# Long convolutions by FFT: the GpSimd instructions moved to the vector engine, two frequency halves joined in one operation

## The chip, the cores and the metric

The kernel runs on one core of a Trainium2 chip. A core has TensorE (PE: matmuls; its weight loads are shown as PEld), VectorE (DVE), ScalarE (ACT), GpSimd (POOL) and SyncE (SP, which here issues nearly all DMAs). Each engine executes its own instructions strictly in the order in which they stand; waits between engines go over semaphores. The metric is the device time of one execution in microseconds. Everything is float32; products that must be exact are formed as three matmuls of split operands.

## The reference, cut to what matters

One layer of a diffusion transformer for 1024 latent tokens and 256 context tokens: input projection, eight attention heads, beside them a Hyena group of 512 channels with two long convolutions in a row, output projection, feed-forward layer. The convolutions are what the change touches:

```python
def _long_conv(u, k_f, bias):
    L = u.shape[1]
    uf = u.astype(jnp.float32)
    y = jnp.fft.irfft(jnp.fft.rfft(uf, n=2 * L, axis=1) * k_f[None], n=2 * L, axis=1)[:, :L]
    return (y + uf * bias.astype(jnp.float32)).astype(u.dtype)

def _hyena(hy, k_f, filt_bias):
    x1, x2, v = jnp.split(hy, 3, axis=-1)
    z = x1 * _long_conv(v, k_f[:, 0], filt_bias[0])
    return x2 * _long_conv(z, k_f[:, 1], filt_bias[1])
```

## The kernel before, in words

The stages in order of time: filters and input projections (to 591 us), attention (first scores at 629 us, last product at 916 us), output projection, feed-forward up and down. The long convolutions, `chain(j)`, lie over the end of the projections and over attention. There are five chains: j = 0 to 3 are 128 latent channels each ("latent chains"), j = 4 is the context with all its channels. Each has two passes, o = 0 and o = 1, one for each convolution in a row; the second needs the result of the first.

A latent pass does this: a forward transform as 8 matmuls (L802) into PSUM tiles `cA`; twiddles, two on ACT (L814, L815) and one on DVE (L816); a butterfly over the four residues (L823 to L828) from tile `Gt` to `X`; the product with the filter spectrum `K` (L837 to L844), which is loaded in two halves into one buffer, so that the second half's load waits until both products of the first half have read; a second butterfly (L849 to L854); twiddles again (L858 to L860); an inverse transform as 8 matmuls (L872); products with the gates (L877 to L885). Pass 1 ends with a store to `hyd`. The index `h` (0, 1) is the half of the 256 frequencies, `i` the real and imaginary part, `q` the residue. Chain 4 has no butterflies and twiddles: ACT copies the transform (L805), and the products follow.

Before the change, part of this is done on GpSimd: L823 for h = 1, L828 for h = 0, the first product L841, three of six steps of the second butterfly (L849, L853, L854), the sum L879 and the last product L885.

The order of the instructions on each engine is not written out. The program is recorded, and a scheduler that plays the program through with a cost model of its own (`schedule_with_timeline_sim=True`) sets the order on all engines together; `chain` is recorded after the projections with a raised priority (`tc.high_priority(offset=CHP)`). So a change of an engine or of an operation's size also changes the places of instructions that are not touched. Chains 0 and 1 have three PSUM banks `cA`, chains 2 to 4 have one.

Attention works on pairs of heads p = 0 to 3: scores (L1021), addition of the bias table `tb` with a row maximum on DVE (L1042), exponentials on ACT (L1055, L1056), transposes (L1065) that DVE and ACT copy in turn (L969, L971), products with the values (L979), scaling into `at` (L1111). The bias tables are loaded by SP with 96 small DMAs for each pair. After attention the load of `w_out` (`wor`, L1149) takes over the memory of the chains and stands on SP behind the last store of `hyd` (L893). In the changed program the lines after L822 have numbers lower by one (L841 is L840, L872 is L871, L1111 is L1110); lines of the first butterfly are L822 to L827.

Of the kernel before, what the change touches and what calls it, by code (L numbers as in the profile page):

```python
# [86 lines left out]
def _build(nc, tc, top, V, A, G, T, Q, I, O, dbg, upto):  # L87
# [20 lines left out]
    def bk(tag):  # L108
        pl, n, bufs = banks[tag]
        return pl.tile([P, 512 * n], F32, tag=tag, name="ps" + tag, bufs=bufs)  # L110
# [22 lines left out]
    def tw_chain(h, r):  # L133
        b = (h * 3 + r - 1) * 3
        return tw[:, b:b + 1], tw[:, b + 1:b + 2], tw[:, b + 2:b + 3]
# [364 lines left out]
    with ies:  # L500
# [3 lines left out]
        for gi, (s, col, tl) in enumerate(groups):  # L504
            xs = []
# [264 lines left out]
    def chain(j):  # L770

        lat = j < 4
        b_ = j % 2

        def s8():
            return cp.tile([P, 2048], F32, tag=f"s8{b_}", name="s8", bufs=2)

        def s4(dt=F32):
            return cp.tile([P, 1024], dt, tag=f"s4{b_}", name="s4", bufs=S4B)

        f4 = "p (h i q c) -> p h i q c"
        v2 = "p (i x) -> p i x"
        src = lxd[j] if lat else cxd
        f1 = "p i x -> p (i x)"

        def load(which):
            t = s4()
            Q.dma_start(out=t, in_=src[which].rearrange(f1))
            return t

        u = load(0)
        for o in range(2):
            uv = u.rearrange(v2, i=2)
            Gt = s8()
            Gv = Gt.rearrange(f4, h=2, i=2, q=4)
            for h in range(2):
                hs = slice(h * P, (h + 1) * P)
                for rp in range(2):
                    pa = bk("cA")
                    xs = slice(rp * 256, (rp + 1) * 256)  # L800
                    for i in range(2):
                        T.matmul(pa[:, i * 256:(i + 1) * 256], dftf[:, i, hs], uv[:, i, xs], start=True, stop=True)  # L802
                    pv = pa.rearrange("p (i r c) -> p i r c", i=2, r=2)
                    if not lat:
                        A.copy(Gv[:, h, :, 2 * rp:2 * rp + 2], pv)  # L805
                        continue
                    for ri in range(2):
                        r = 2 * rp + ri
                        if r == 0:
                            A.copy(Gv[:, h, :, 0], pv[:, :, 0])  # L810
                            continue
                        c, s, ns = tw_chain(h, r)
                        t = cp.tile([P, 2, P], F32, tag=f"t{b_}", name="t", bufs=TB)
                        A.activation(t[:, 0], pv[:, 1, ri], AF.Copy, scale=ns)  # L814
                        A.activation(t[:, 1], pv[:, 0, ri], AF.Copy, scale=s)  # L815
                        V.scalar_tensor_tensor(Gv[:, h, :, r], pv[:, :, ri], c, t, op0=ALU.mult, op1=ALU.add)  # L816
            if lat:
                ac = s4().rearrange(f4, h=2, i=2, q=2)
                X = s8()
                Xv = X.rearrange(f4, h=2, i=2, q=4)  # L820
                Xf = X.rearrange("p (h x c) -> p h x c", h=2, x=8)
                for h in range(2):  # L822
                    (G if h else V).tensor_add(ac[:, h], Gv[:, h, :, 0:2], Gv[:, h, :, 2:4])  # L823
                    V.tensor_sub(Gv[:, h, :, 2:4], Gv[:, h, :, 0:2], Gv[:, h, :, 2:4])
                    V.tensor_sub(Xf[:, h, 2:8:5], Gv[:, h, :, 2], Gv[:, h, ::-1, 3])
                    V.tensor_add(Xf[:, h, 3:7:3], Gv[:, h, :, 2], Gv[:, h, ::-1, 3])
                    V.tensor_add(Xv[:, h, :, 0], ac[:, h, :, 0], ac[:, h, :, 1])  # L827
                    (V if h else G).tensor_sub(Xv[:, h, :, 1], ac[:, h, :, 0], ac[:, h, :, 1])  # L828
                Y = Gt
            else:  # L830
                X = Gt
                Y = s8()
            Xs = X.rearrange("p (h i x) -> p h i x", h=2, i=2)
            Ys = Y.rearrange("p (h i x) -> p h i x", h=2, i=2)
            for h in range(2):
                Kt = cp.tile([P, 2, 512], F32, tag=f"K{b_}", name="K", bufs=1)
                Q.dma_start(out=Kt.rearrange(f1), in_=(Kd[o, j] if lat else Kc[o])[:, h * 1024:(h + 1) * 1024])  # L837
                kr = Kt[:, 0:1].to_broadcast([P, 2, 512])
                ki = Kt[:, 1:2].to_broadcast([P, 2, 512])
                B = s4().rearrange(v2, i=2)  # L840
                G.tensor_mul(B, Xs[:, h, ::-1], ki)  # L841
                V.tensor_mul(Ys[:, h], Xs[:, h], kr)
                V.tensor_sub(Ys[:, h, 0], Ys[:, h, 0], B[:, 0])
                V.tensor_add(Ys[:, h, 1], Ys[:, h, 1], B[:, 1])  # L844
            if lat:
                ac = s4().rearrange(f4, h=2, i=2, q=2)
                Gf = Gt.rearrange("p (h x c) -> p h x c", h=2, x=8)
                for h in range(2):
                    G.tensor_add(ac[:, h], Gv[:, h, :, 0:4:2], Gv[:, h, :, 1:4:2])  # L849
                    V.tensor_sub(Xv[:, h, :, 0:2], Gv[:, h, :, 0:4:2], Gv[:, h, :, 1:4:2])  # L850
                    V.tensor_add(Gf[:, h, 1:8:6], Xv[:, h, :, 0], Xv[:, h, ::-1, 1])
                    V.tensor_sub(Gf[:, h, 3:6:2], Xv[:, h, :, 0], Xv[:, h, ::-1, 1])
                    G.tensor_add(Gv[:, h, :, 0], ac[:, h, :, 0], ac[:, h, :, 1])  # L853
                    G.tensor_sub(Gv[:, h, :, 2], ac[:, h, :, 0], ac[:, h, :, 1])  # L854
                    for r in (1, 2, 3):
                        c, s, ns = tw_chain(h, r)
                        t = cp.tile([P, 2, P], F32, tag=f"t{b_}", name="t", bufs=TB)
                        A.activation(t[:, 0], Gv[:, h, 1, r], AF.Copy, scale=s)  # L858
                        A.activation(t[:, 1], Gv[:, h, 0, r], AF.Copy, scale=ns)
                        V.scalar_tensor_tensor(Gv[:, h, :, r], Gv[:, h, :, r], c, t, op0=ALU.mult, op1=ALU.add)  # L860
            if o == 0:
                x1 = load(1).rearrange(v2, i=2)
                un = s4()
            else:
                x2 = load(2).rearrange(v2, i=2)
                ot = s4().rearrange(v2, i=2)
            for rp in range(2):
                pa = bk("cA")
                xs = slice(rp * 256, (rp + 1) * 256)
                for i in range(2):  # L870
                    for h in range(2):  # L871
                        T.matmul(pa[:, i * 256:(i + 1) * 256], idft[:, i, h], Ys[:, h, i, xs], start=h == 0,  # L872
                                 stop=h == 1, skip_group_check=True)
                pv = pa.rearrange(v2, i=2)
                tt = cp.tile([P, 2, 2, 256], F32, tag=f"s4{b_}", name="tt", bufs=S4B)
                if o == 0:
                    V.tensor_mul(tt[:, 0], pv, x1[:, :, xs])  # L877
                    V.tensor_mul(tt[:, 1], pv, x1[:, ::-1, xs])
                    G.tensor_add(un.rearrange(v2, i=2)[:, :, xs], tt[:, :, 0], tt[:, :, 1])  # L879
                else:  # L880
                    yt = tt[:, 0, 0]
                    A.copy(yt, pv[:, 0])
                    V.tensor_sub(ot[:, 0, xs], yt, pv[:, 1])
                    V.tensor_add(ot[:, 1, xs], yt, pv[:, 1])
                    G.tensor_mul(ot[:, :, xs], ot[:, :, xs], x2[:, :, xs])  # L885
            if o == 0:
                u = un
            elif lat:
                for i in range(2):
                    Q.dma_start(out=hyd[i * 4:i * 4 + 4, :, j * P:(j + 1) * P].rearrange("r p c -> p r c"),  # L890
                                in_=ot[:, i].rearrange("p (r c) -> p r c", r=4))
            else:
                Q.dma_start(out=hyd[8:10].rearrange("i p x -> p i x"), in_=ot)  # L893

    for j in range(5):
        if j == 2:
            cbk.close()
            cbk = Banks("bkd", "right", "tile", cA=(1, 1))
        with tc.high_priority(offset=CHP):
            chain(j)  # L900
# [319 lines left out]
    ot = wo_.tile([P, 512], F32, tag="ot", name="ot", bufs=1)  # L1220
# [296 lines left out]
    for f in range(NFF):  # L1517
# [7 lines left out]
        i, cs = f // 2, slice(f % 2 * 256, f % 2 * 256 + 256)  # L1525
# [77 lines left out]
    B = {(r, b): wdn[:, :, r, b] for r in range(2) for b in range(2)}  # L1603
# [53 lines left out]
    xs = {}  # L1657
# [107 lines left out]
```

## Time and profile before

| | us |
|---|---|
| median of three runs (lowest, highest) | 1921.23 (1920.3, 1921.35) |
| the profiled execution | 1918.35 |
| its span, first to last instruction | 1916.6 |
| busy: PE, DVE, ACT, POOL | 1748.7, 1372.6, 885.0, 412.4 |
| mean granted clock of TensorE | 0.947 |

In the profile a row of a group gives line, engine, operation, result and operands by the names of the program, shapes and count; then busy time in us and mean duration in ns; then the idle time of the engine just before, and what ended it. A row of the timeline starts with the start and the duration in us and may end with the idle time before it and its releaser in brackets. A row of stretches gives start and end, length, and the busy time (with the number of instructions) of PE, PEld, DVE, ACT and POOL, then the granted clock, the share of DMA and GB/s. A row of waits names who waited for whom: us in total, times, longest. A matmul of 128x256 shows as two records (x4 is two matmuls).

### The profile page before, as it was taken

To read this page: it belongs to the slowest core of one execution; us is meant where nothing else is said; L and a number is where in the kernel's file an instruction comes from. 1 tells how busy PE (TensorE), PEld (TensorE's weight loads), DVE (VectorE), ACT (ScalarE), POOL (GpSimd) and SP (SyncE) were. 2 spreads that over 40 slices of the span, in tenths; PEclk is the share of its full clock that TensorE was granted. 3 is DMA by queue.
4 is the path that set the end of the run, shared out by engine and by line. 5 is a ranking of instruction groups with operands and counts; after the bars stand their busy time and mean duration, and the time that the engine had idled before them with its cause. 6 is when DMAs were issued, how large, how long until landed. Compare 5 with 4: busy or idle time off the path is not lost.

```text
span 1916.6 us, 27816 instructions
## 1 busy us (share of the span) xinstructions
PE 1748.7 (91%) x9999; PEld 1468.5 (77%) x9999; DVE 1372.6 (72%) x2175; ACT 885.0 (46%) x1827; POOL 412.4 (22%) x331
## 2 busy tenths in 40 slices
PE   5899989999994789789899699999999999999998
PEld 1688877887773345445688599999999999788786
DVE  4667648747777776776455888888877777656887
ACT  4654435434333355455555544444444444443352
POOL 2354546543654322233100000000000000000001
PEclk7999989999997799799899799999999999999999
DMA  7424444455433334421622154555322222853663
GB/s 266 133 75 129 130 128 119 143 170 170 139 111 122 84 96 94 108 63 56 209 99 100 57 161 163 164 168 173 114 72 73 72 62 71 286 184 109 207 209 127
DMA packets 238267, 249.80 MB, mean 130 GB/s; under 512 B 56610, under 2 KB 187795, under 8 KB 237873
## 3 DMA queue, kind: packets, MB, share of 16 engines
q1 hardware_dynamic: 236168, 247.09, 41.2%
q8 instruction: 79, 1.29, 0.3%
q10 hardware_dynamic: 1705, 0.82, 0.2%
q14 instruction: 59, 0.48, 0.1%
q0 software_dynamic: 256, 0.11, 0.0%
HBM read 176.75 MB, written 71.20 MB: 129 GB/s over the span
## 4 chain that ended last, share of the span: by engine, by line
PE 36%; DVE 10%; DMA 6%; issue 3%; ACT 3%; POOL 1%; SPq 0%; DVEq 0%; POOLq 0%; ACTq 0%
PE psd L118 6%; PE psd L116 6%; PE psd L117 6%; PE psa L116 2%; PE psa L117 2%; PE psa L118 2%; DMA wt<-in_w_down_dram 2%; DMA tdr<-wt 2%; PE psc L117 1%; PE psc L118 1%; PE psc L116 1%; PE psb L117 1%; PE psb L118 1%; PE psb L116 1%; DVE cv L1514 1%
## 5 line engine op out<-in xcount | busy, mean ns | idle before, releaser
L116 PE MATMUL psp<-hh,wh 128*128 128x512 f32 (+1 forms) x552 | 203.1, 368 | 2.3 <-ACT wh L121 1.9
L117 PE MATMUL psp<-hl,wh 128*128 128x512 f32 (+1 forms) x552 | 201.1, 364 | 0.0
L118 PE MATMUL psp<-hh,wl 128*128 128x512 f32 (+1 forms) x552 | 200.3, 363 | 0.0
L1680 POOL TENSOR_TENSOR rs<-rs,mhalf 128x1 f32<-128x1 f32 x10 | 7.7, 770 | 812.5 <-DVE rs L1679 812.5
L116 PE MATMUL psa<-T,ws 128*128 128x256 f32 (+1 forms) x528 | 166.1, 315 | 3.1 <-ACT rows L1480 3.0
L117 PE MATMUL psa<-T,ws 128*128 128x256 f32 (+1 forms) x528 | 165.6, 314 | 2.8 <-DVE T L1207 2.8
L118 PE MATMUL psa<-T,ws 128*128 128x256 f32 (+1 forms) x528 | 165.0, 313 | 0.0
L116 PE MATMUL psd<-wd,gs 128*128 128x512 f32 x360 | 140.5, 391 | 3.1 <-ACT gs L121 3.1
L117 PE MATMUL psd<-wd,gs 128*128 128x512 f32 x360 | 140.9, 391 | 0.0
L118 PE MATMUL psd<-wd,gs 128*128 128x512 f32 x360 | 124.9, 390 | 1.6 <-DVE gs L122 1.6
L116 PEld LDWEIGHTS psp<-hh,wh 128*128 128x128 f32 x552 | 106.5, 193 | 23.7 <-issue 7.0
L117 PEld LDWEIGHTS psp<-hl,wh 128*128 128x128 f32 x552 | 106.7, 193 | 15.0 <-issue 1.2
L116 PE MATMUL psc<-T,ws 128*128 128x384 f32 (+1 forms) x352 | 110.3, 313 | 8.4 <-ACT ws L121 8.4
L118 PEld LDWEIGHTS psp<-hh,wl 128*128 128x128 f32 x552 | 106.0, 192 | 14.9 <-issue 0.8
L117 PE MATMUL psc<-T,ws 128*128 128x384 f32 (+1 forms) x352 | 110.3, 313 | 0.0
L118 PE MATMUL psc<-T,ws 128*128 128x384 f32 (+1 forms) x352 | 110.1, 313 | 0.0
L117 PE MATMUL psb<-T,ws 128*128 128x384 f32 (+1 forms) x352 | 109.7, 312 | 0.0
L118 PE MATMUL psb<-T,ws 128*128 128x384 f32 (+1 forms) x352 | 109.6, 311 | 0.0
L116 PE MATMUL psb<-T,ws 128*128 128x384 f32 (+1 forms) x352 | 109.5, 311 | 0.0
L116 PEld LDWEIGHTS psa<-T,ws 128*128 128x128 f32 x528 | 101.4, 192 | 4.6 <-ACT rows L1480 4.5
L117 PEld LDWEIGHTS psa<-T,ws 128*128 128x128 f32 x528 | 101.5, 192 | 3.1 <-DVE T L1207 3.1
L118 PEld LDWEIGHTS psa<-T,ws 128*128 128x128 f32 x528 | 101.1, 192 | 0.0
(391 smaller groups left out, 4821.2 us busy)
## 6 DMA issues: line engine op xcount, KB each, us to landing
wada<-in_w_ada_dram SPq DMA_DIRECT2D x48, 512.0 KB
wr<-in_w_up_dram SPq DMA_DIRECT2D x44, 512.0 KB
gr<-gdr SPq DMA_DIRECT2D x44, 320.0 KB
wr<-in_w_in_dram SPq DMA_DIRECT2D x23, 512.0 KB
wt<-in_w_down_dram SPq DMA_DIRECT2D x44, 256.0 KB
tdr<-wt SPq DMA_DIRECT2D x44, 256.0 KB
gdr<-cv SPq DMA_DIRECT2D x22, 512.0 KB
wr<-tdr SPq DMA_DIRECT2D x20, 512.0 KB
```

Source lines behind the costliest of these rows:

```text
L116: T.matmul(out, ah, bh, start=start, stop=False, skip_group_check=True)
L117: T.matmul(out, ah, bl, start=False, stop=False, skip_group_check=True)
L118: T.matmul(out, al, bh, start=False, stop=stop, skip_group_check=True)
L1514: V.scalar_tensor_tensor(cv, r[:, 2:NC + 2], ffw(2, ch), cv, op0=ALU.mult, op1=ALU.add)
L1680: G.tensor_tensor(rs, rs, mhalf, op=ALU.pow)
```

## The change

All instructions of `chain` that ran on GpSimd are issued on VectorE, and in both butterflies of a latent pass the loop over the two halves h is gone: one operation of twice the size takes both. The loop over h remains for the product with `K` and for the twiddles behind the second butterfly.

```diff
-                for h in range(2):
-                    (G if h else V).tensor_add(ac[:, h], Gv[:, h, :, 0:2], Gv[:, h, :, 2:4])
-                    V.tensor_sub(Gv[:, h, :, 2:4], Gv[:, h, :, 0:2], Gv[:, h, :, 2:4])
-                    V.tensor_sub(Xf[:, h, 2:8:5], Gv[:, h, :, 2], Gv[:, h, ::-1, 3])
-                    V.tensor_add(Xf[:, h, 3:7:3], Gv[:, h, :, 2], Gv[:, h, ::-1, 3])
-                    V.tensor_add(Xv[:, h, :, 0], ac[:, h, :, 0], ac[:, h, :, 1])
-                    (V if h else G).tensor_sub(Xv[:, h, :, 1], ac[:, h, :, 0], ac[:, h, :, 1])
+                V.tensor_add(ac, Gv[:, :, :, 0:2], Gv[:, :, :, 2:4])
+                V.tensor_sub(Gv[:, :, :, 2:4], Gv[:, :, :, 0:2], Gv[:, :, :, 2:4])
+                V.tensor_sub(Xf[:, :, 2:8:5], Gv[:, :, :, 2], Gv[:, :, ::-1, 3])
+                V.tensor_add(Xf[:, :, 3:7:3], Gv[:, :, :, 2], Gv[:, :, ::-1, 3])
+                V.tensor_add(Xv[:, :, :, 0], ac[:, :, :, 0], ac[:, :, :, 1])
+                V.tensor_sub(Xv[:, :, :, 1], ac[:, :, :, 0], ac[:, :, :, 1])
...
-                G.tensor_mul(B, Xs[:, h, ::-1], ki)
+                V.tensor_mul(B, Xs[:, h, ::-1], ki)
...
+                V.tensor_add(ac, Gv[:, :, :, 0:4:2], Gv[:, :, :, 1:4:2])
+                V.tensor_sub(Xv[:, :, :, 0:2], Gv[:, :, :, 0:4:2], Gv[:, :, :, 1:4:2])
+                V.tensor_add(Gf[:, :, 1:8:6], Xv[:, :, :, 0], Xv[:, :, ::-1, 1])
+                V.tensor_sub(Gf[:, :, 3:6:2], Xv[:, :, :, 0], Xv[:, :, ::-1, 1])
+                V.tensor_add(Gv[:, :, :, 0], ac[:, :, :, 0], ac[:, :, :, 1])
+                V.tensor_sub(Gv[:, :, :, 2], ac[:, :, :, 0], ac[:, :, :, 1])
                 for h in range(2):
-                    G.tensor_add(ac[:, h], Gv[:, h, :, 0:4:2], Gv[:, h, :, 1:4:2])
-                    V.tensor_sub(Xv[:, h, :, 0:2], Gv[:, h, :, 0:4:2], Gv[:, h, :, 1:4:2])
-                    V.tensor_add(Gf[:, h, 1:8:6], Xv[:, h, :, 0], Xv[:, h, ::-1, 1])
-                    V.tensor_sub(Gf[:, h, 3:6:2], Xv[:, h, :, 0], Xv[:, h, ::-1, 1])
-                    G.tensor_add(Gv[:, h, :, 0], ac[:, h, :, 0], ac[:, h, :, 1])
-                    G.tensor_sub(Gv[:, h, :, 2], ac[:, h, :, 0], ac[:, h, :, 1])
...
-                    G.tensor_add(un.rearrange(v2, i=2)[:, :, xs], tt[:, :, 0], tt[:, :, 1])
+                    V.tensor_add(un.rearrange(v2, i=2)[:, :, xs], tt[:, :, 0], tt[:, :, 1])
...
-                    G.tensor_mul(ot[:, :, xs], ot[:, :, xs], x2[:, :, xs])
+                    V.tensor_mul(ot[:, :, xs], ot[:, :, xs], x2[:, :, xs])
```

The program has 8 instructions more on DVE (2185 for 2177) and 104 fewer on POOL (229 for 333); PE, ACT and SP have the same instructions in another order.

The first place is PE at the end of the attention, before the change. `pscA` are the transforms of the chains (L802 forward, L872 inverse), `psX` transposes and row scalings of attention, `psav` its products with the values; L1170 begins the stage that follows.

```order
L872 MATMUL pscA<-s_6432,idft 128x256 x4
L979 MATMUL psav<-pt,vs 64x256 x2
L1065 MATMUL psX<-ident,Pl_6518 128x128 x2
L1065 MATMUL psX<-ident,Pl_6522 128x128 x2
L979 MATMUL psav<-pt,vs 64x256 x2
L989 MATMUL psX<-ident,lrow_6500 128x128
...
L994 MATMUL psX<-lt,sel 128x128 x4
L1170 MATMUL psX<-ones_71,asq 128x2
```

And the same place in the changed program:

```order
L871 MATMUL pscA<-s_6147,idft 128x256 x4
L978 MATMUL psav<-pt,vs 64x256 x2
L988 MATMUL psX<-ident,lrow_6404 128x128
...
L993 MATMUL psX<-lt,sel 128x128 x4
L1169 MATMUL psX<-ones_71,asq 128x2
L1169 MATMUL psX<-ones_71,sq 128x2
...
L802 MATMUL pscA<-s_6264,dftf 128x256 x8
L871 MATMUL pscA<-s_6283,idft 128x256 x8
L802 MATMUL pscA<-s_6300,dftf 128x256 x8
L871 MATMUL pscA<-s_6336,idft 128x256 x8
L1169 MATMUL psX<-ones_71,asq 128x2
```

Before, the first row is the end of chain 4, and attention matmuls stand behind it. Now the first row is the end of chain 3, and all four transforms of chain 4 stand together behind the last matmul of attention.

The second place is DVE at the same moment, first before the change (`at` is attention's last product, `tt` and `s` belong to chain 4), then in the changed program.

```order
L883 TENSOR_TENSOR s_6449<-tt,pscA 128x256
L884 TENSOR_TENSOR s_6449<-tt,pscA 128x256
L1111 TENSOR_TENSOR at_6483<-psav,bs 128x2x16x16
L1136 COPY sh_8562<-mods 128x16
L1173 TENSOR_SCALAR ria<-psX 128x2
```

```order
L884 TENSOR_TENSOR s_6241<-s_6241,s_6239 128x2x256
L1110 TENSOR_TENSOR at_6387<-psav,bs 128x2x16x16
L840 TENSOR_TENSOR s_6286<-s_6266,K 128x1024
L841 TENSOR_TENSOR s_6283<-s_6266,K 128x1024
L842 TENSOR_TENSOR s_6283<-s_6283,s_6286 128x512
L843 TENSOR_TENSOR s_6283<-s_6283,s_6286 128x512
...
L882 TENSOR_TENSOR s_6353<-tt,pscA 128x256
L883 TENSOR_TENSOR s_6353<-tt,pscA 128x256
L884 TENSOR_TENSOR s_6353<-s_6353,s_6351 128x2x256
L1135 COPY sh_8466<-mods 128x16
```

All 28 DVE instructions of chain 4, from the first product with K to the last gate, now stand behind attention's last product.

The third place is PE where the projections (`psp`) end and attention begins (`psS`, scores); the chains here are chain 1 (and one forward transform of chain 2, right ahead of the scores). Before:

```order
L118 MATMUL psp<-hh,wl 128x256
L225 MATMUL pstB<-wada_7_5270,silc 32x256 x4
...
L677 MATMUL pstB<-ident,fo 128x128 x2
L732 MATMUL pstB<-ident,ck 128x128 x2
L872 MATMUL pscA<-s_5715,idft 128x256 x8
L802 MATMUL pscA<-s_5848,dftf 128x256 x2
L1021 MATMUL psS<-k,q 128x264 x2
```

And now:

```order
L118 MATMUL psp<-hh,wl 128x256
L871 MATMUL pscA<-s_5566,idft 128x256
...
L871 MATMUL pscA<-s_5566,idft 128x256 x3
L677 MATMUL pstB<-ident,fo 128x128 x2
L871 MATMUL pscA<-s_5566,idft 128x256 x3
L802 MATMUL pscA<-s_5660,dftf 128x256 x2
L732 MATMUL pstB<-ident,ck 128x128 x2
L802 MATMUL pscA<-s_5660,dftf 128x256 x6
L871 MATMUL pscA<-s_5679,idft 128x256 x8
L802 MATMUL pscA<-s_5800,dftf 128x256 x2
L1020 MATMUL psS<-k,q 128x264 x2
```

Before, only the inverse transform of chain 1's pass 1 stands between projections and scores. Now the inverse transform of its pass 0 and the forward transform of its pass 1 stand there as well.

## The prediction

> **What bounds the kernel now.** I read the page first, then the busy time by stretches, then the waits of PE, then the timeline around the places where the changed lines stand.
>
> ```profile
> span 1916.6 us, 27816 instructions
> PE 1748.7 (91%) x9999; PEld 1468.5 (77%) x9999; DVE 1372.6 (72%) x2175; ACT 885.0 (46%) x1827; POOL 412.4 (22%) x331
> ```
>
> PE is the bound of the whole, but the long convolutions run from 436 to 913 us, beside the end of the input projections and the whole attention. There the stretches differ (PE, PEld, DVE, ACT, POOL busy, then the granted clock):
>
> ```profile
> 440.00:591.00 151.00, 140.47 (x738) 113.71 (x736) 115.42 (x164) 55.91 (x132) 79.19 (x51) 0.94 0.40 123
> 600.00:628.90 28.90, 8.31 (x22) 5.00 (x22) 20.09 (x34) 5.32 (x15) 17.85 (x32) 0.57 0.50 145
> 628.90:728.60 99.70, 76.67 (x394) 43.52 (x393) 78.86 (x177) 48.81 (x167) 32.47 (x23) 0.85 0.39 96
> 728.60:769.90 41.30, 38.38 (x258) 24.41 (x257) 26.31 (x52) 26.43 (x83) 6.19 (x5) 1.00 0.40 97
> 769.90:848.90 79.00, 58.63 (x321) 34.14 (x321) 58.70 (x123) 38.32 (x125) 28.08 (x20) 0.85 0.36 89
> 848.90:915.80 66.90, 63.52 (x373) 39.65 (x373) 42.38 (x97) 35.44 (x109) 21.32 (x10) 0.97 0.18 56
> ```
>
> The first row is the projections, the second the gap before attention, the other four the head pairs 0 to 3. PE is full in the projections and in pairs 1 and 3, and has holes in the gap and in pairs 0 and 2. What PE waits for in the first two stretches:
>
> ```profile
> PE pscA L872 <- POOL s L853: 3.6, 1, 3.6
> PE pscA L872 <- DVE s L860: 3.1, 2, 2.6
> PE pscA L872 <- DVE s L860: 15.9, 2, 14.4
> ```
>
> The first two rows are from 440 to 591 us, the third from 600 to 630. So GpSimd is rarely what PE waits for directly; what it does to Vector shows in the groups (busy us, mean ns):
>
> ```profile
> L842 DVE TENSOR_TENSOR s<-s,K 128x1024 f32<-128x1024 f32 x20 | 41.1, 2055 | 4.0 <-DMA K<-Kc 3.2 <-ACT s L805 0.5
> L844 DVE TENSOR_TENSOR s<-s,s 128x512 f32<-128x512 f32 x20 | 22.9, 1143 | 0.0
> L843 DVE TENSOR_TENSOR s<-s,s 128x512 f32<-128x512 f32 x20 | 21.1, 1053 | 11.7 <-POOL s L841 11.6
> L850 DVE TENSOR_TENSOR s<-s 128x512 f32<-128x512 f32 x16 | 14.8, 926 | 0.0
> L824 DVE TENSOR_TENSOR s<-s 128x512 f32<-128x512 f32 x16 | 12.9, 806 | 2.4 <-POOL s L823 2.2
> ...
> L841 POOL TENSOR_TENSOR s<-s,K 128x1024 f32<-128x1024 f32 x20 | 58.6, 2929 | 58.0 <-DVE s L826 18.3 <-ACT s L805 16.6 <-issue 11.8
> L849 POOL TENSOR_TENSOR s<-s 128x512 f32<-128x512 f32 x16 | 24.4, 1527 | 0.6 <-DVE s L844 0.6
> L885 POOL TENSOR_TENSOR s<-s,s 128x512 f32<-128x512 f32 x10 | 13.1, 1312 | 58.3 <-issue 42.5 <-DVE s L884 15.8
> ```
>
> **Part 1, the work that moves to Vector.** Undisturbed prices on Vector, and what surrounds them at the end of attention:
>
> ```profile
> 893.39 1.22 DVE L842 TENSOR_TENSOR s<-s,K 128x1024 f32<-128x1024 f32 x1 [0.20 <-ACT s L805]
> 896.88 0.69 DVE L843 TENSOR_TENSOR s<-s,s 128x512 f32<-128x512 f32 x1 [0.33 <-POOL s L841]
> 896.77 1.13 PE L802 MATMUL pscA<-s,dftf 128*128 128x256 f32 x4
> 897.94 0.59 ACT L805 COPY s<-pscA 128x512 f32<-128x512 f32 x1 [1.00 <-PE pscA L802]
> 896.87 3.75 DMA K<-Kc
> 900.78 3.37 POOL L841 TENSOR_TENSOR s<-s,K 128x1024 f32<-128x1024 f32 x1 [3.93 <-DMA K<-Kc]
> 906.81 0.37 ACT L882 COPY tt<-pscA 128x256 f32<-128x256 f32 x1 [1.87 <-PE pscA L872]
> 907.22 0.42 DVE L883 TENSOR_TENSOR s<-tt,pscA 128x256 f32<-128x256 f32 x1 [1.05 <-ACT tt L882]
> 908.91 1.89 PE L872 MATMUL pscA<-s,idft 128*128 128x256 f32 x8
> 912.12 1.27 POOL L885 TENSOR_TENSOR s<-s,s 128x512 f32<-128x512 f32 x1 [2.75 <-DVE s L884]
> 913.41 2.78 DMA hyd<-s
> 915.14 0.69 DVE L1111 TENSOR_TENSOR at<-psav,bs 128x512 f32<-128x512 f32 x1 [3.10 <-ACT bs L996]
> 916.33 0.81 SPq L1149 DMA_DIRECT2D wor<-in_w_out_dram  x2
> ```
>
> So 1024, 512 and 256 elements cost 1.22, 0.69 and 0.42 us. What GpSimd did becomes, at these prices, 20 x 1.22 (L841) + 16 x 0.69 (L849) + 32 x 0.42 (L853, L854) + 8 x 0.69 (L823) + 8 x 0.42 (L828) + 20 x 0.69 (L879, L885) = 71.5 us. Each joined pair saves about 0.15 us (2 x 0.69 - 1.22, 2 x 0.42 - 0.69); 12 pairs in 8 latent passes give 14.5. Vector gets 57 us more. Against it stands the stretch: the five Vector rows above hold 112.8 us, and 40 operations at 0.69, 20 at 1.22 and 32 at 0.69 would be 74, so 39 us vanish with GpSimd's work. Vector's own load rises by at most 18 us over 475; smaller groups that are stretched too may bring that to nothing. It is no gain in itself, and no loss: what decides is where the work stands now.
>
> **Part 2, the start of attention.** The rows of the order show that the inverse transform of pass 0 of chain 1 no longer stands inside the projections: 8 + 8 + 8 matmuls of chain 1 now come after the last projection matmul.
>
> ```profile
> 590.85 0.28 PE L118 MATMUL psp<-hh,wl 128*128 128x256 f32 x1
> 618.24 1.19 PE L872 MATMUL pscA<-s,idft 128*128 128x256 f32 x2 [14.39 <-DVE s L860]
> 623.01 0.48 DVE L860 SCALAR_TENSOR_TENSOR s<-s,tw,t 128x256 f32<-128x256 f32 x1 [0.89 <-ACT t L859]
> 628.91 1.20 PE L1021 MATMUL psS<-k,q 64*128 64x264 f32 x8
> ```
>
> The projections get shorter by the waits of 3.6 and 3.1 us and by 16 matmuls of 0.53 (a row of x4 is two matmuls, 1.03 to 1.13 us): 15 us. From their end to the first scores it was 38 us. Now the serial list is: three last twiddles at 1.4 (0.48 and the wait of 0.89 for ACT), two inverse blocks at 1.9 with their products at 1.4 and a sum, 12; a forward transform and six twiddles, a little under 8; butterfly 2 x 1.22 + 4 x 0.69 = 5; products 2 x (2 x 1.22 + 2 x 0.69) = 7.6, and between them the reload of K of 3.9, of which 1.4 lies behind the two subtractions, 10; butterfly 5; six twiddles at 1.4, 8; inverse transform 2 and the forward one ahead of the scores 1: about 50 us. So 15 less and 12 more. I take 0; from -12 (the memsets of GpSimd no longer delay the butterfly) to +12 (Vector, held by the K reload, keeps the projections' results waiting).
>
> **Part 3, attention with one chain less.** Chain 4 (the context) leaves pair 3, where PE is busy 63.5 of 66.9 us. Its 32 matmuls at 0.53 are 17 us. Another 3 us I take from Vector's waits for GpSimd in attention:
>
> ```profile
> DVE s L843 <- POOL s L841: 6.7, 7, 1.8
> ...
> L842 DVE TENSOR_TENSOR s<-s,K 128x1024 f32<-128x1024 f32 x12 | 23.1, 1927 | 3.9 <-DMA K<-Kc 3.2 <-ACT s L805 0.5
> L843 DVE TENSOR_TENSOR s<-s,s 128x512 f32<-128x512 f32 x12 | 10.6, 882 | 6.8 <-POOL s L841 6.7
> L844 DVE TENSOR_TENSOR s<-s,s 128x512 f32<-128x512 f32 x12 | 10.3, 859 | 0.0
> ```
>
> Together -20 (half of that wait, since PE has holes only in two pairs of four). At best the whole wait and the stretch of these three rows (44.0 less 12 x 1.22 and 24 x 0.69, 13 us) come off the holes of pairs 0 and 2: -37. At worst Vector's added work lands in the holes and the gain of PE is lost behind it: +8.
>
> **Part 4, the tail.** In the changed order chain 4 stands whole after the last attention product, on PE, ACT and DVE alike. Before, it ended (912.12 + 1.27 = 913.4) 2.4 us ahead of attention (915.14 + 0.69 = 915.8), and w_out's load follows the landing of hyd. Its length alone, with one PSUM bank and one K buffer, from the end of attention: ACT squares at for 1.1 us first; two transform pairs (1.05) and copies (0.59) with handovers until 3.7; products and K's release at 6.1 (2 x 1.22); reload 3.9; second half 1.22 x 2 + 0.69 x 2, at 13.4 (neighbours on Vector overlap by 0.1); four inverse matmuls 1.9, two products 1.4, the same again, and the sum: 20.9. Pass 1: transform from 20.4, first half at 24.0, K free at 26.3, reload to 30.2, second half to 33.7, inverse 2.0, copy 0.37, difference and sum 0.8, product 0.69, the second block the same: 41.7. So w_out comes 41.7 + 2.4 = +44 us later than attention's end did before. Nothing covers it: all later work of the output projection needs w_out, which needs this hyd. Bounds: +36 if handovers cost nothing, +50 if PE's 12 us in it run at the clock of 0.57 that the gap had. Afterwards PE's order is the old one: 0.
>
> **The sum.** 0 - 20 + 44 = +24 us on the profiled execution's 1918.35 us (span 1916.6 and 1.75 around it): 1942.4. That execution lies 2.9 below the median of 1921.23, so the forecast is 1945 us.
>
> **Rivals.** *The freed Vector wins* (0.14): stretch and waits for GpSimd were on the path in pairs 0 and 2, so part 3 gives its full -37 and part 2 its -12, against a tail of 36: -13, 1908 us, faster. For it speaks that L842 takes 2055 ns on average against 1220 alone; against it that PE's listed waits for chain results are short but for the one of 14.4. The Trainium skill, page "SBUF — State Buffer", section "SBUF: two separate sides", supports it: Vector operations with two SBUF inputs and GpSimd operations that read SBUF exclude each other for the whole instruction. The trace agrees with stretched rows on both sides (L841 2929 ns).
>
> *It cancels* (0.07): -34 and -8 against +44: 1923 us.
>
> *Vector's queue is blocked as well* (0.14): all butterflies and products now stand in one queue, and the K reload stops it for 3.9 - 1.4 = 2.5 us per pass; eight latent passes are 20 us, behind which attention's maxima and copies queue. It decides if these waits fall while PE has nothing in store. 24 + 20 to 28: about 1969 us.
>
> That the change is not carried out is excluded: GpSimd keeps 229 of 333 instructions, none of a chain.
>
> **How the numbers follow.** The forecast has 0.65, its own range 1928 to 1963. Slower is forecast and blocked queue, 0.79; no change (within 0.2%, which is about what can be told here) 0.07; faster 0.14. The range of 8 in 10 leaves out most of the first rival and takes in the blocked queue's centre: 1918 to 1970.
>
> **What would show it.** Chain 4's transforms after the last L1110, with PE nearly idle for 40 us and w_out's load more than 20 us later than 916 show part 4; if that stretch is under 30 us, the tail is mis-sized. Attention from first scores to last product in 287 - 20 us shows part 3; under 250 the first rival holds, over 295 the third. The first scores near 629 show part 2. L842's counterpart at 1.22 us shows that the stretch is gone. The forecast is wrong if the load of w_out starts before 925.

## The result, and the profile after

The changed kernel takes 1950.32 us (median of 4 runs, 1947.16 to 1953.98) against 1921.29 for the kernel before (4 runs, 1920.3 to 1922.8): ratio 1.0151, 95% interval 1.0132 to 1.0170. It is slower by about 29 us; the forecast was 1945 with a range of 1918 to 1970. The profiled execution is the shortest of the four.

The head of its page, the span and the busy times:

```profile
span 1945.3 us, 27592 instructions
PE 1739.3 (89%) x9999; PEld 1458.2 (75%) x9999; DVE 1372.1 (71%) x2183; ACT 885.5 (46%) x1827; POOL 256.7 (13%) x227
```

Vector's busy time is what it was (1372.1 for 1372.6), though it now does what kept GpSimd busy for 156 us (412.4 less 256.7). The stretches of the changed kernel: projections; from their last matmul (570.4) to the first scores; attention to its last product (904.1); from there to w_out's load (948.7):

```profile
440.00:570.40 130.40, 129.42 (x725) 105.79 (x724) 99.40 (x150) 51.35 (x121) 26.29 (x14) 1.00 0.47 146
570.40:624.10 53.70, 17.74 (x74) 11.66 (x73) 34.67 (x66) 15.88 (x43) 6.46 (x22) 0.71 0.40 108
624.10:904.10 280.00, 213.20 (x1284) 125.31 (x1284) 195.60 (x426) 143.91 (x472) 0.00 (x0) 0.91 0.29 73
904.10:948.70 44.60, 19.46 (x62) 11.91 (x60) 21.46 (x28) 6.38 (x11) 0.00 (x0) 0.84 0.23 77
```

Against before (first scores 628.9, attention 286.9, w_out 0.5 us behind it, 1000.3 from there to the end) the first scores come 4.8 us earlier, attention is 6.9 shorter, the tail is 44.1 longer, and the rest is 3.7 shorter (1945.3 - 948.7 = 996.6): 28.7 us in all. In the tail PE is busy for 19.5 of 44.6 us. Its first and last rows, with one stop inside:

```profile
903.39 0.69 DVE L1110 TENSOR_TENSOR at<-psav,bs 128x512 f32<-128x512 f32 x1 [1.20 <-ACT bs L995]
913.72 1.23 DVE L840 TENSOR_TENSOR s<-s,K 128x1024 f32<-128x1024 f32 x1 [2.55 <-DMA K<-Kc]
945.07 0.69 DVE L884 TENSOR_TENSOR s<-s,s 128x512 f32<-128x512 f32 x1
945.79 0.37 SPq L892 DMA_DIRECT2D hyd<-s  x1
948.70 6.45 SPq L1148 DMA_DIRECT2D wor<-in_w_out_dram  x4
```

The groups whose rows on Vector were stretched before (L842 2055, L844 1143, L843 1053 ns), under their new numbers, and the two first steps of a joined butterfly:

```profile
L840 DVE TENSOR_TENSOR s<-s,K 128x1024 f32<-128x1024 f32 x20 | 24.6, 1229 | 52.0 <-DMA K<-Kd 40.5 <-ACT s L805 6.4 <-DMA K<-Kc 5.0
L841 DVE TENSOR_TENSOR s<-s,K 128x1024 f32<-128x1024 f32 x20 | 24.4, 1218 | 0.0
L842 DVE TENSOR_TENSOR s<-s,s 128x512 f32<-128x512 f32 x20 | 15.8, 789 | 0.3
L843 DVE TENSOR_TENSOR s<-s,s 128x512 f32<-128x512 f32 x20 | 13.7, 684 | 0.0
L822 DVE TENSOR_TENSOR s<-s 128x1024 f32<-128x1024 f32 x8 | 10.9, 1361 | 0.2
L823 DVE TENSOR_TENSOR s<-s 128x1024 f32<-128x1024 f32 x8 | 9.9, 1241 | 0.2
```

The stretch is gone, as forecast (L842 with 789 ns on average keeps a little of it). But the first row has something new: Vector stands still for 40.5 us, waiting for K of the latent chains (`Kd`), where before it waited 3.2 us for K in all, and only for the context's. 29.2 us of it lie in attention, three stops of 9.0 to 10.7. The longest, on SP (rows SPq, whose second number is the length of the whole run of issues) and Vector:

```profile
650.37 12.50 SPq L958 DMA_DIRECT2D tb<-rpw  x27
651.24 1.22 DVE L841 TENSOR_TENSOR s<-s,K 128x1024 f32<-128x1024 f32 x1
662.97 0.37 SPq L836 DMA_DIRECT2D K<-Kd  x1
666.80 1.23 DVE L840 TENSOR_TENSOR s<-s,K 128x1024 f32<-128x1024 f32 x1 [10.65 <-DMA K<-Kd]
```

The product L841 gives the buffer of K free at 652.5. The reload stands on SP behind a run of 27 loads of the bias table and is issued 10.5 us later; 3.8 us after that the second product starts. Attention's own Vector work stands behind it.

### The profile page after: what moved, and what is told of

Read it like the earlier page. It is cut to its first block, busy times and chain, and to the rows that moved or that the text cites. A ratio compares the mean times of both kernels' runs of the same rounds, so it can differ in the third digit from the quotient of the medians.

```text
span 1945.3 us, 27592 instructions
## 1 busy us (share of the span) xinstructions
PE 1739.3 (89%) x9999; PEld 1458.2 (75%) x9999; DVE 1372.1 (71%) x2183; ACT 885.5 (46%) x1827; POOL 256.7 (13%) x227
## 3 DMA queue, kind: packets, MB, share of 16 engines
q1 hardware_dynamic: 236168, 247.09, 40.5%
## 4 chain that ended last, share of the span: by engine, by line
PE 55%; DVE 15%; DMA 11%; ACT 5%; SPq 5%; issue 5%; POOL 3%; DVEq 0%; POOLq 0%; ACTq 0%
PE psd L118 6%; PE psd L116 6%; PE psd L117 6%; SPq L958 4%; PE psp L118 4%; PE psp L116 4%; PE psp L117 4%; PE psa L116 2%; PE psa L117 2%; PE psa L118 2%; DMA wt<-in_w_down_dram 2%; PE psav L978 2%; PE psc L116 2%; PE psc L117 2%; PE psc L118 2%
```

## The experiments

The theory after the first look (A): the tail is the cost, and it is a matter of order; moving the work costs nothing. The rival (B): Vector's queue is stopped by the reload of K wherever the products stand on Vector. The change has two halves, so the first two runs do each alone. The diffs are against the kernel before or the changed kernel, as said; a ratio is to the kernel before, timed beside the run.

**Move only.** The kernel before, all operations of the chains on Vector, the loops over h left as they were:

```diff
-                    (G if h else V).tensor_add(ac[:, h], Gv[:, h, :, 0:2], Gv[:, h, :, 2:4])
+                    V.tensor_add(ac[:, h], Gv[:, h, :, 0:2], Gv[:, h, :, 2:4])
...
-                G.tensor_mul(B, Xs[:, h, ::-1], ki)
+                V.tensor_mul(B, Xs[:, h, ::-1], ki)
...
```

> The kernel before with every GpSimd operation of the chains put on Vector, the loops over h kept as they were (so 71.5 us of Vector work at undisturbed prices and no joined operation). In its order chain 4 stands inside attention again: its last transform ends right behind the last attention matmul. Theory A (the tail costs the time, moving by itself costs nothing): time within 10 us of before, 1911 to 1931, w_out's load less than 12 us behind attention's last product. Theory B (Vector's queue is stopped by the reloads of K wherever the products stand on Vector; in the changed kernel it waits 29 us for K during attention): the waits for K in attention are 25 us or more again and the time is 1940 or more.

Measured: 1902.97 us, ratio 0.9920 (0.9904 to 0.9936). Moving the work is not free, it gains 15 us. Its stretches, cut as above:

```profile
440.00:574.80 134.80, 133.61 (x748) 109.23 (x751) 111.60 (x196) 54.51 (x129) 28.08 (x14) 1.00 0.46 141
574.80:609.80 35.00, 13.38 (x56) 8.81 (x53) 28.62 (x67) 12.01 (x34) 6.43 (x22) 0.66 0.51 150
609.80:897.70 287.90, 228.52 (x1340) 137.72 (x1340) 217.52 (x499) 149.16 (x481) 0.00 (x0) 0.90 0.32 83
897.70:903.90 6.20, 1.25 (x6) 0.76 (x4) 1.44 (x3) 1.43 (x2) 0.00 (x0) 0.96 0.23 85
```

Attention is as long as before (287.9 for 286.9). The gain lies ahead of it: the projections end at 574.8 instead of 591.1. Before, PE paused three times in them, for 3.60 us (GpSimd, L853), 3.21 us (DVE, L229) and 2.63 us (DVE, L860); here its longest wait is 1.0 us. The ten-microsecond slices that hold the three pauses or the end of one, first of before, then of the moved kernel:

```profile
466.00:476.00 10.00, 7.47 (x29) 6.23 (x30) 6.66 (x13) 5.04 (x14) 2.31 (x3) 0.83 0.28 90
516.00:526.00 10.00, 7.21 (x29) 5.24 (x30) 8.12 (x10) 5.37 (x14) 7.35 (x7) 0.66 0.39 120
556.00:566.00 10.00, 6.79 (x32) 6.04 (x31) 10.00 (x13) 1.47 (x5) 8.37 (x7) 0.71 0.57 185
```

```profile
466.00:476.00 10.00, 10.00 (x64) 8.42 (x60) 7.62 (x21) 6.78 (x17) 0.00 (x0) 1.00 0.38 123
516.00:526.00 10.00, 8.96 (x40) 7.19 (x41) 7.71 (x14) 5.02 (x15) 2.38 (x1) 1.00 0.57 181
556.00:566.00 10.00, 10.00 (x53) 8.22 (x50) 8.96 (x22) 4.92 (x14) 0.00 (x0) 1.00 0.56 176
```

With each pause the granted clock falls too (0.83, 0.66, 0.71; without the pauses it is 1.00 in all three slices): the projections had 10.5 us of idle PE and 7 us of slower matmuls (PE busy 140.6 for 133.6 here, with six records more now). The Trainium skill, page "TensorE: Matmul & The Clock Gate", section "HAM oscillation — how this bites in real kernels", warns of PE pauses above about 3.4 us; the clock does fall behind 3.60 us here, but the slice with the pause of 2.63 (two stops of 0.2 and 0.4 us stand just ahead of it) has the lowest of all, 0.66.

Vector does not wait for a latent chain's K anywhere in this run. Why, the rows of the same pass show (chain 2, pass 0):

```profile
625.99 1.22 DVE L841 TENSOR_TENSOR s<-s,K 128x1024 f32<-128x1024 f32 x1
627.12 1.22 DVE L842 TENSOR_TENSOR s<-s,K 128x1024 f32<-128x1024 f32 x1
628.86 0.37 SPq L837 DMA_DIRECT2D K<-Kd  x1
633.21 0.48 DVE L816 SCALAR_TENSOR_TENSOR s<-pscA,tw,t 128x256 f32<-128x256 f32 x1
635.23 0.47 DVE L816 SCALAR_TENSOR_TENSOR s<-pscA,tw,t 128x256 f32<-128x256 f32 x1
641.06 1.21 DVE L841 TENSOR_TENSOR s<-s,K 128x1024 f32<-128x1024 f32 x1
```

With the loops over h kept, half 0 goes through butterfly and product while half 1 is still being transformed and twiddled (L816 at 633 and 635). From the start of the one product to that of the other it is 15 us, and the reload runs in them. Joined, the first butterfly has to wait for both halves; then the two products follow each other directly, with the reload between them.

**Join only.** The butterflies joined, GpSimd keeps its part:

```diff
+                V.tensor_add(ac, Gv[:, :, :, 0:2], Gv[:, :, :, 2:4])
...
+                G.tensor_sub(Xv[:, :, :, 1], ac[:, :, :, 0], ac[:, :, :, 1])
...
                 G.tensor_mul(B, Xs[:, h, ::-1], ki)
```

> Butterflies with both halves joined, but GpSimd keeps its part: the first product with K, three of the six steps of the second butterfly and one of the first, the sum and the last product. In its order all of chain 4 stands behind attention, as in the changed kernel. Theory A (the tail, whatever engine does the work): a tail of about 50 us (GpSimd's products at 2.9 instead of 1.2 us on the way) and a time of 1945 to 1965. Theory B (Vector's queue stopped by K): GpSimd takes the wait for K, Vector is free, and the time is within 10 us of before, 1911 to 1931.

Measured: 1959.91 us, ratio 1.0213 (1.0198 to 1.0229), with the tail of the forecast's kind:

```profile
639.00:907.80 268.80, 215.11 (x1283) 126.75 (x1283) 192.98 (x394) 144.13 (x472) 62.16 (x33) 0.92 0.29 75
907.80:961.50 53.70, 26.30 (x64) 15.64 (x62) 14.19 (x21) 6.38 (x11) 19.36 (x9) 0.64 0.22 69
```

A's numbers came out, B's did not; GpSimd did not take the wait either (Vector waits 27.4 us for `Kd`). So the change is a gain of 15 us and a loss of 44 in one (41 where GpSimd keeps its part): moving is worth taking, joining is not.

**Chain 4 ahead of chain 3,** in the changed kernel:

```diff
-    for j in range(5):
+    for j in (0, 1, 2, 4, 3):
```

> The changed kernel with one edit: chain 4 is recorded ahead of chain 3. In its order chain 4 and most of chain 3 stand inside attention; only the last inverse transform of chain 3 with its products (about 8 us) stands behind it. Theory A: the tail shrinks from 44.6 to about 10 us, attention gets chain 4's 32 matmuls back (17 us) as PE has room: 1950 - 35 + 0 to 17 = 1915 to 1932. Theory B: attention takes five or six waits for K of about 10 us instead of three; what the tail gives back is lost there: 1940 to 1955.

Measured: 1949.19 us, ratio 1.0163 (1.0139 to 1.0188): no gain. A's expectation fell, and B's number came out for a reason that B does not give (attention has three waits for `Kd`, 18.9 us in all, not five or six of 10):

```profile
628.10:920.70 292.60, 229.93 (x1329) 135.56 (x1328) 199.60 (x427) 145.24 (x468) 0.00 (x0) 0.89 0.29 76
920.70:954.20 33.50, 7.90 (x16) 4.87 (x16) 19.10 (x29) 6.07 (x15) 0.00 (x0) 0.57 0.15 47
```

The tail is still 33.5 us. I had read from the order that only one inverse transform stands behind attention; but the middle of that pass, on Vector and ACT, runs behind it as well. Another chain came last, and the end stayed. So the tail is not chain 4's: it is the end of the row of chains.

**K loaded by GpSimd,** in the changed kernel:

```diff
-                Q.dma_start(out=Kt.rearrange(f1), in_=(Kd[o, j] if lat else Kc[o])[:, h * 1024:(h + 1) * 1024])
+                G.dma_start(out=Kt.rearrange(f1), in_=(Kd[o, j] if lat else Kc[o])[:, h * 1024:(h + 1) * 1024])
```

> The changed kernel with one edit: the loads of K are issued by GpSimd, which has nothing else to do in attention, instead of SP, where they stand behind up to 27 loads of the bias tables. Chain 4 stays whole behind attention. Theory A (waits of Vector for K lie beside other work): attention's 280 us change by less than 5, time 1943 to 1953. Theory B (they are on the path): the three waits of 9 to 11 us fall to about 3 and attention gets some 15 to 20 us shorter, time 1928 to 1938; the waits that remain in the tail stay at 2.5.

Measured: 1956.53 us, ratio 1.0203 (1.0186 to 1.0220), slower than the changed kernel, which neither theory allowed:

```profile
620.00:884.60 264.60, 205.94 (x1265) 122.49 (x1264) 185.84 (x407) 139.78 (x458) 3.69 (x7) 0.91 0.30 76
884.60:957.20 72.60, 39.14 (x81) 23.55 (x81) 33.43 (x50) 11.50 (x25) 1.58 (x3) 0.56 0.15 51
```

The waits for `Kd` fell from 40.5 to 17.1 us, and attention got 15 us shorter, as B said. The tail took it back and more: the scheduler now set the end of chain 3 behind attention too. What shortens attention alone gains nothing.

This gave a third theory (C): the five chains, ten passes one behind the other, are the path from 440 us to w_out's load. In every run so far the transforms of one pass end before those of the next begin, but for chains 0 and 1 around 526 us. The end of the last inverse transform (the last row of L872, or its new number) then has to fix the time:

| kernel | end of last inverse transform | span | difference |
|---|---|---|---|
| before | 910.8 | 1916.6 | 1005.8 |
| changed | 943.8 | 1945.3 | 1001.5 |
| move only | 898.9 | 1898.5 | 999.6 |
| join only | 956.0 | 1959.0 | 1003.0 |
| chain 4 before 3 | 948.8 | 1953.4 | 1004.6 |
| K by GpSimd | 952.0 | 1954.3 | 1002.3 |

The spans differ by up to 60 us, the differences by 6.2. The end of attention does not fix the time in this way: from it to the end of the span it is 1000.8 us before and 1041.2 in the changed kernel. The table shows that the total follows the end of the row; what makes the row longer it does not show. The run with K on GpSimd is a warning here: Vector waits 23 us less for `Kd`, but the row is not shorter. From the first forward to the last inverse transform of chains 2 and 3 it takes 284.0 us, where the changed kernel takes 277.1. How much of a wait for K the row feels cannot be read from the wait alone.

Theory D against C: each joined operation costs its share.

**First butterfly joined only; second only.** All work on Vector, one of the two blocks as in the change, the other per half:

> All chain work on Vector; the first butterfly (ahead of the products with K) joined, the second one per half as before. Theory C (the five chains in a row are the path from 440 us to the load of w_out, and joining the first butterfly puts both products with K behind both halves of the transform, so that the second half's load of K, which can only start when the first product has read, comes onto that path): Vector waits 30 us or more for K, the chain is as long as in the changed kernel, 1940 to 1955. Theory D (each joined butterfly costs its share): about half way between 1903 and 1950, 1920 to 1933.

> All chain work on Vector; the first butterfly per half, the second one joined. Theory C: the product of half 0 stands ahead of half 1's transform again, the load of K is covered (Vector waits under 8 us for it in all), and only the second butterfly's staggering is lost: 1900 to 1915. Theory D: 1920 to 1933.

Measured: 1930.36 us, ratio 1.0070 (1.0047 to 1.0093), for the first, 1915.15, ratio 0.9985 (0.9970 to 0.9999), for the second. Against the move alone (0.9920) they cost some 29 and 12 us. The first has chain 4 behind attention and 31.9 us of waits for `Kd`; the second has neither (0.7 us):

```profile
617.80:882.40 264.60, 210.75 (x1284) 125.43 (x1284) 196.20 (x450) 143.92 (x473) 0.00 (x0) 0.92 0.30 76
882.40:932.20 49.80, 29.67 (x63) 17.43 (x61) 22.03 (x29) 6.37 (x11) 0.00 (x0) 0.55 0.22 74
```

```profile
606.80:899.10 292.30, 230.16 (x1331) 136.70 (x1330) 214.09 (x471) 148.78 (x480) 0.00 (x0) 0.91 0.32 81
899.10:911.40 12.30, 5.45 (x14) 3.59 (x14) 4.05 (x8) 1.80 (x3) 0.00 (x0) 0.58 0.12 44
```

C is right on which join exposes K. On the size C was wrong for the first, which lies in D's range, and the second lies 0.15 us above the upper edge of C's; the two add up to 41 of the 44 us that both cost together (1.0151 less 0.9920). From the end of the last inverse transform to the span's end it is 1000.0 and 1000.3 us here, so the rule of the table holds.

**One load of K per pass,** in the changed kernel:

```diff
-                Kt = cp.tile([P, 2, 512], F32, tag=f"K{b_}", name="K", bufs=1)
-                Q.dma_start(out=Kt.rearrange(f1), ...)
+                if h == 0:
+                    Kt = cp.tile([P, 2, 512], F32, tag=f"K{b_}", name="K", bufs=1)
+                    Q.dma_start(out=Kt.rearrange(f1), ...)
```

> The changed kernel, both butterflies joined, but each pass loads only the first half of K and uses it for both halves of the frequencies (so half of K's 10 MB is not read and the product is another). Theory C in the form that the reload of K is the whole cost of joining (40 us of Vector's waits for K): 1905 to 1920. Theory C in the form that the lost staggering itself costs, every stage of a pass now waiting for both halves: the waits for K go, the time stays at 1932 to 1948.

Measured: 1930.72 us, ratio 1.0069 (1.0042 to 1.0096). No wait for K is left, and by the ratios 16 of the 44 us between move only and the changed kernel go with it (the spans say 17). The other 28 remain: they are joining without the reload. The time lies between the ranges of C's two forms, 1.3 us below the second. (The edit also leaves out ten DMAs; a second buffer for K would be the cleaner test, and no run here has one.)

Where the other 28 may lie, the transforms on PE show. First, last forward and first inverse rows of chain 2, pass 0, in the moved kernel and then in the changed one:

```profile
608.75 1.10 PE L802 MATMUL pscA<-s,dftf 128*128 128x256 f32 x4 [1.34 <-ACT tt L882]
629.99 1.18 PE L802 MATMUL pscA<-s,dftf 128*128 128x256 f32 x4
651.94 0.60 PE L872 MATMUL pscA<-s,idft 128*128 128x256 f32 x2
```

```profile
623.09 1.10 PE L802 MATMUL pscA<-s,dftf 128*128 128x256 f32 x4 [1.43 <-DVE s L883]
634.47 1.03 PE L802 MATMUL pscA<-s,dftf 128*128 128x256 f32 x4
681.80 0.70 PE L871 MATMUL pscA<-s,idft 128*128 128x256 f32 x2
```

Half by half, 20.8 us lie between the forward transform and the inverse one, since the butterflies and products of one half run beside the transform of the other; joined, it is 46.3. The same measure over the four passes of chains 2 and 3, and what it does to the row:

| kernel | between the transforms, four passes | chains 2 and 3, first forward to last inverse | chain 4, the same |
|---|---|---|---|
| move only | 82.2 | 236.3 | 51.9 |
| changed | 168.0 | 277.1 | 40.4 |
| changed, one load of K | 123.3 | 266.5 | 42.2 |
| changed, K by GpSimd | 119.2 | 284.0 | 47.8 |

Without any wait for K the joined passes still have 41 us more between their transforms than the moved ones, and the two chains take 30 us longer. Chain 4, which has no butterflies, takes less time behind attention than in it. The first column does not give the row by itself: with K on GpSimd it is the shortest of the three joined kernels and the row the longest, since there the transforms themselves take longer.

**Half of the bias loads by GpSimd,** in the moved kernel without joins:

```diff
-                Q.dma_start(out=tv[:, :, a * 8:a * 8 + 64], in_=rpw[var, :, h, :, d * 8:d * 8 + 64])
+                (G if half else Q).dma_start(out=tv[:, :, a * 8:a * 8 + 64], in_=rpw[var, :, h, :, d * 8:d * 8 + 64])
```

> The kernel with the work moved but nothing joined (run before at 1903 us), with one edit: half of the bias table loads are issued by GpSimd instead of SP. There Vector waits 19.7 us for bias tables in attention and PE 12.1 us for q, which SP issues behind them. If SP's issues (0.46 us each, 96 for a pair of heads) hold up attention: 1890 to 1899. If the chains alone are the path (theory C) or GpSimd's issues are dearer: 1900 to 1912.

Measured: 1900.51 us, ratio 0.9908 (0.9880 to 0.9937), not to be told from the move alone (0.9904 to 0.9936). Vector's waits for the bias tables fall from 19.7 to 1.4 us and nothing is gained. Attention gets 9 us shorter (608.2 to 886.8), but Vector now waits 9.1 us for `Kd`, and the last inverse transform ends only 4 us earlier (895.0 for 898.9): most of these waits lay beside the row of chains.

**Two chains abreast.** The direct test of C: chains 2 and 3 are recorded in turn, stage by stage, so that one fills the pauses of the other. `chain` gets a `yield` behind the forward transform, the middle and the products:

```diff
+    for js in ((0,), (1,), (2, 3), (4,)):
...
+        gs = [chain(j) for j in js]
+        while gs:
+            for g in list(gs):
+                with tc.high_priority(offset=CHP):
+                    if next(g, 1):
+                        gs.remove(g)
```

Three kernels with it: the changed one, the moved one without joins, and the kernel before; a fourth is the moved one with chains 0 and 1 abreast as well.

> The changed kernel with chains 2 and 3 recorded in turn, stage by stage (forward transform, middle, inverse transform, products), so that one fills the pauses of the other; chain 4 after them. In its order all chains end at about five sixths of attention. Theory C (the row of chains is the path; joining costs because it makes each pass longer): the cost of joining vanishes, w_out is loaded a few us behind attention's last product, and the time falls from 1950 to 1885 to 1905. Theory E (joining costs through the engines' queues, whatever the chains' place: Vector held by K's reload with attention's maxima behind it): Vector's waits for K of 30 us or more stay, and the time stays above 1925.

> The same recording in turn of chains 2 and 3 with the work moved to Vector but nothing joined. Theory C: chains are off the path here as well, so the time is within 12 us of the joined one of the same recording, 1885 to 1905. Theory E: 25 us or more below it.

> The kernel before (GpSimd keeps its share) with chains 2 and 3 recorded in turn. Theory C: where the row of chains isn't the path, moving work off GpSimd isn't worth 15 us any more: 1885 to 1910, within 12 us of the other two. If moving gains by the Vector time that is stretched beside GpSimd even so: 10 us or more above the moved one.

> Moved, nothing joined, chains 0 and 1 in turn and chains 2 and 3 in turn. Theory C: chains 0 and 1 are partly beside each other already (their transforms interleave at 520 to 536 us), and the pause of PE between the projections and the first scores (35 us in the moved kernel) shortens to 15 to 25: 1875 to 1895. If what holds the start of attention is the load of the bias tables and of q, as late as before: 1890 to 1905.

| two abreast | us | ratio to before (interval) | first scores | attention | last inverse transform ends |
|---|---|---|---|---|---|
| changed | 1915.47 | 0.9993 (0.9979 to 1.0008) | 626.2 | 291.9 | 883.3 |
| moved | 1901.46 | 0.9916 (0.9899 to 0.9932) | 612.9 | 295.5 | 857.9 |
| before | 1924.68 | 1.0031 (1.0019 to 1.0043) | 630.3 | 299.2 | 877.2 |
| moved, also 0 and 1 | 1904.48 | 0.9929 (0.9912 to 0.9945) | 603.9 | 303.9 | 822.4 |

The stretches of attention of the changed and of the moved one, chains 2 and 3 abreast:

```profile
626.20:918.10 291.90, 232.76 (x1345) 138.93 (x1344) 223.48 (x463) 158.11 (x490) 0.00 (x0) 0.91 0.34 95
```

```profile
612.90:908.40 295.50, 232.59 (x1345) 141.84 (x1344) 228.20 (x513) 157.52 (x492) 0.00 (x0) 0.90 0.37 102
```

All four end the chains inside attention, and w_out's load starts ahead of attention's end: no tail. For the changed kernel this takes away 30 us (1.0151 to 0.9993), as much as the change had cost; so that cost did lie on the row of chains, which is C's main point. Theory E's sign, waits for `Kd` of 30 us or more, did not come: they fell to 21.9, so the new order took some of them away as well. But C's stronger claims fell: of the four times only that of the moved kernel lies in C's range. The kernels are not within 12 us of each other: joined and moved differ by 15, and 13.3 of these stand in the first scores (626.2 for 612.9), where chains 0 and 1 still run one behind the other. Moving is worth some 22 us here too, 17.4 of them ahead of the first scores. And with the chains out of the way nothing is gained over the move alone (0.9920): attention itself takes 292 to 304 us with all chains inside it. With chains 0 and 1 abreast as well, the pause of PE between the projections and the first scores did shorten to 17.7 us, as C expected, but the projections end 8.5 us later (586.2 for 577.7) and attention is 8.4 longer, so that nothing is left. What holds attention there was not followed further.

## Why the prediction was right, point by point

The forecast of slower held, and the time lay 5 us above it. Its sum by stages was 0 - 20 + 44 + 0; the profiled execution shows -4.8 - 6.9 + 44.1 - 3.7. That the total is so near is in part luck: attention was 13 us dearer than forecast, and 8.5 of them came back in two stages for which nothing was forecast.

*Part 1, the work that moves.* The stretch did vanish, and by more than the 39 us of the five rows: Vector's busy time is 1376.9 us with the move alone (+4.3, where 71.5 less 39 would be +32), so nearly all of the 71.5 us of new work is paid by operations that are no longer stretched by GpSimd. In the changed kernel it is -0.5, where up to +18 was allowed. The Trainium skill's rule behind the first rival (page "SBUF — State Buffer", section "SBUF: two separate sides") agrees: with the chains' GpSimd operations gone, the second product with K (L842, now L841) takes 1218 ns on average, where it took 2055. Joining saved 4.8 us of Vector's busy time (1376.9 less 1372.1), not 14.5. The step that failed is the conclusion "no gain in itself, and no loss". Moving gained 15 us, through PE pauses in the projections and the clock lost with them; part 2 counted these waits at their bare 6.7 us.

*Part 2, the start of attention.* The projections' last matmul came 20.7 us earlier (570.1 for 590.85; 15 forecast) and the gap grew to 54 us (50 forecast); -4.8 lies within the -12 to +12 given. The inverse transform of chain 1 waits 29.1 us there, of which Vector's stop for K is 7.1.

*Part 3, attention.* -6.9 in place of -20, within -37 to +8. The term that was mis-sized is the reload of K: part 2 and the third rival priced it at 3.9 us from the release, 2.5 of them uncovered. It took up to 14.3 (10.5 until SP issued it, 3.8 to the product), since the place of the reload in SP's row, behind 27 bias loads, was not looked at. With one load of K per pass attention is 269.3 us, 17.6 less than before, which is nearly the -20. The third rival's mechanism was thus there, at 16 us (the run with one load of K), beside the main one and not instead of it.

*Part 4, the tail.* Chain 4's last product ends 41.7 us behind attention's (945.76 less 904.08), as the sum had it, and w_out's load comes 44.6 us behind it; the reload waits of 2.4 and 2.6 were as listed. PE's clock in it was 0.84, so the bound of +50 was not reached (12 us of PE at 0.57 would be 9 more, +53, not +50). The size was right; the reading of it as a cost of its own was not. Moving another chain to the end left the time where it was, and the tail is what the row of ten passes overhangs attention.

*The first rival* (the freed Vector wins, 1908) named a mechanism that the move alone shows (1903), in another place: in the projections, not in pairs 0 and 2, whose attention did not get shorter. It lost because the change brought joining along. What no part of the prediction had is what joining does to the order within a pass: that product and reload of half 0 no longer run under the transform of half 1. In the prediction joining was only a saving of 14.5 us. It costs 44: 16 by the reload, the other 28 with the loads of K halved. That these 28 are stages waiting for both halves is what the longer stretch between the transforms suggests, and it is not shown by a run; only the reload's part was measured by one.

*What stays open.* All these prices hold for the order that the scheduler sets: with two chains abreast 30 of the 44 us go. The time from w_out's load to the end varies between 994.6 and 1000.3 us in the kernels without chains abreast, though the work there is the same; it was not looked into. Nor was what keeps attention at 292 us and more when the chains end early.

## What to carry to other kernels

Joining two halves into one larger operation saves an issue, but where the halves run staggered it also takes away the time under which a single buffer is reloaded; look for the reload's place in the issuing queue before believing that it is covered. When several serial pieces share one buffer, compare the end of the last of them over all variants: if it moves with the total, the row is the path, and a tail behind another stage is only where it shows. Then break the row, as here with two chains abreast, to see how much of the cost goes. Split a change that has two halves and run each: here one gains 15 us and the other loses 44.

## What the runs showed of the hardware

PE pauses of 2.6 to 3.6 us in an otherwise full stage went with a granted clock of 0.66 to 0.83 over the ten microseconds around them (1.00 without them); three pauses of 9.4 us in all went with a stage that was 16 us longer. A queue that issues many small loads (0.46 us each on SP) delays a load of which another engine's whole queue is in need by as much as 10.5 us, though the DMA engines are only 29% busy in that stage. And work taken from GpSimd that is 71.5 us at Vector's undisturbed prices (an estimate from its rows) added 4.3 us to Vector's busy time.
